# An encoder layer on one Trainium2 core: where the branches' forms are made, and when their weights and the first gate's products come

## The chip, the cores and the metric

The kernel runs on one NeuronCore of a Trainium2 chip. The metric is device time in microseconds (us) of one execution, the median of several. The engines are TensorE (PE: matmuls and transposes, results in PSUM), VectorE (DVE), ScalarE (ACT), GpSimd (POOL; here element-wise work on SBUF and a few DMA issues) and SyncE (SP, which issues the weight fetches). Each engine takes its own instructions strictly in the order of the program; they wait for each other by semaphores.

## The reference, cut to what matters

One layer on 512 tokens of width 1024: a mixer, a cross-attention into 256 memory tokens and a SwiGLU, each behind an RMS norm and added to the residual. The change touches the mixer:

```
p = h @ w_in                    # h: normed x, 512 x 1024
q, k, v, z, cb, cc, cx, gates = split(p)
ya = stick_breaking_attention(q, k, v)
u, v = split(gelu(z)); v = layer_norm(v, ln_g, ln_b)
yb = u * (w_spatial @ v + b_spatial)     # the spatial unit: 4 groups of 128 channels, 128 positions
yc = cb * conv3(cc * cx)
merged = sum over n of sigmoid(gates[n]) * (y[n] @ w_branch[n])
out = merged @ w_out
```

## The kernel before

**Arithmetic.** Matmuls are in fp32r. Each fp32 operand is cut in two: `wh` is the cast (ACT), `wl` the remainder, operand minus cast (DVE); `split` and `cut` write both. A product is three matmuls: high x high, high x low, low x high. `hT` (pair `hTh`, `hTl`) is the normed input, transposed, 8 row blocks x 512 tokens.

**Buffers.** Raw weights come by SP into `wr`, a ring of three 1 MB tiles in the pool `wp`. Their halves go into `wh` and `wl`, rings of six each. PSUM has eight banks: four turn about in `bank()`, four are the accumulators `acc`.

**The order** on each engine is made by a scheduler from the program's order and its own estimate of times; what is wrapped in `pin(...)` keeps its place.

**The spatial unit.** `nat_gemm` multiplies four token tiles of 128 rows by a 1024 x 512 weight (two raw tiles, four pieces of two row blocks). First come the columns of v (`sgu_v`): Gelu, statistics, the scale on DVE, gain and bias on POOL with `lng` and `lnb`, and the cut into `vlh`, `vll`. Then `w_spatial` (`wsr`) is transposed (`pws`) and cut into `wsh`, `wsl`. Then come the columns of u (`sgu_u`): a Gelu of each tile into `un`. Then `pg`, the spatial product of each of four groups, is multiplied into `un` on DVE, and `sgu_turn` transposes `un` (`pgt`) into `yb` (`ybh`, `ybl`).

**The branches.** Twelve items (three branches x four pieces of 256 gate columns) compute a gate and a branch product each. The first item's gate is a plain product (`gts`, two column tiles). The other eleven run in `seven_run` by a scheme of seven half-size products in place of eight. It needs sums and differences of the quarters of the weights (made per item) and of `hT` (made once, the "forms" t1 to t4). `right_forms(k)` makes the forms of row blocks k and k + 4: POOL adds `hTh` and `hTl` back into fp32, four DVE subtractions make the forms, and a cast and a remainder write them to `hTth`, `hTtl`. Its work tile `f` has eight parts and is taken from the ring `wr`. It is called for k = 0 to 3 behind the Gelus of the u tiles.

An item's branch product `pbr` (`extra_mul`, 24 matmuls) uses its piece of `w_branch`, fetched into `wb` and cut by `extra_cut`. Behind the last item the output product `pb` begins, in four accumulators.

Of the kernel before, what the change touches and what calls it, by code (L numbers as in the profile page):

```python
# [17 lines left out]
def encoder_kernel(  # L18
# [9 lines left out]
    nc = tc.nc  # L28
# [108 lines left out]
    def gemm(dst, lh, ll, rh, rl, ks, first=True, last=True):  # L137

        n, tot = 0, 3 * len(ks)
        for a, b in ((lh, rh), (lh, rl), (ll, rh)):  # L140
            for i, j in ks:
                nc.tensor.matmul(dst, a(i), b(j), start=first and n == 0, stop=last and n == tot - 1)  # L142
                n += 1
# [3 lines left out]
        gemm(dst, lambda i: w[0][:, i, :], lambda i: w[1][:, i, :],  # L147
             lambda i: act[0][:, i, cs], lambda i: act[1][:, i, cs], [(i, i) for i in range(k)])

    def nat_gemm(w, col0, act, ntt, evac, raws=(None, None), ready=None):  # L150

        pieces = []
        for c in range(2):
            pieces += w_rows(w, 4 * c, 4, col0, raws[c])
        if ready is not None:
            ready()
        for t in range(ntt):
            dst = bank(nm("pn"))
            gemm(dst,
                 lambda i: act[0][:, i, t * P:(t + 1) * P], lambda i: act[1][:, i, t * P:(t + 1) * P],  # L160
                 lambda i: pieces[i // 2][0][:, i % 2, :], lambda i: pieces[i // 2][1][:, i % 2, :],
                 [(i, i) for i in range(KD)])
            evac(t, dst)

    ALLT = slice(0, T)
# [143 lines left out]
    def seven_run(items, fill=lambda i: None, at=None, then=None):  # L309

        z = len(items)
        for k in range(z + 1):
            n = items[k] if k < z else None
            p = items[k - 1] if k else None
            q = items[k + 1] if k + 1 < z else None
            if k == at:
                got = then()
            if k + 2 < z:
                items[k + 2].load()
            if n:  # L320
                n.a, n.c = n.tile_a(), n.tile_a()
                n.mul(n.a, "l11", "r11", True, False)
            if q:
                q.sums()
            if n:
                y = n.hi(("s3", "l22"), n.right)
                n.m1 = n.keep("m1")
                n.lo(y)
                n.mul(n.c, "s1", "t1", True, False)
            if k == z:  # L330
                fill(0)
            if p:
                p.gate22()
                p.mul(p.c, "s4", "r22", False, True)
            if k == z:
                fill(1)
            if q:
                x = q.hi(("l11", "l12"), q.left)
                q.lo(x)
                c = q.hi(("s1",), q.s1)  # L340
            if p:
                p.c12(p.c[:, 0:256], p.u2)
            if n:
                n.mul(n.a, "s2", "t2", False, False)
                n.u2 = n.keep("u2")
            if q:
                q.sums2()
                q.lo(c)
            if k > 1:
                items[k - 2].extra_out()  # L350
            if p:
                p.done0()
                p.mul(p.a, "l22", "t4", False, True)
            if q and not q.late:
                b = q.hi(("s2", "s4"), q.left)
            if p:
                p.c21(p.a[:, 0:256])
                p.extra_cut()
            if n:
                n.extra_load()  # L360
                bk = bank(nm("pfb"))
                n.mul(bk, "l12", "r21", True, True)
            if q and q.late:
                n.c11(bk[:, 0:256], n.m1)
                b = q.hi(("s2", "s4"), q.left)
            if q and k:
                q.lo(b)
            if n:
# [12 lines left out]
        return got if then else None  # L381
# [273 lines left out]
    vl = tuple(up.tile([P, NT, W], F32R, name=f"vl{s}") for s in "hl")  # L655

    def sgu_v(t, dst):
        zt = up.tile([P, W], F32, name=nm("zt"), tag="zt", bufs=2)
# [5 lines left out]
        rs = rstd_of(mv[:, 1:2], 1e-5, 1.0)  # L664
        nc.vector.tensor_scalar(out=zt, in0=zt, scalar1=mv[:, 0:1], scalar2=rs, op0=ALU.subtract, op1=ALU.mult)
        nc.gpsimd.tensor_tensor(out=zt, in0=zt, in1=lng, op=ALU.mult)
        nc.gpsimd.tensor_tensor(out=zt, in0=zt, in1=lnb, op=ALU.add)
        split(zt, vl[0][:, t, :], vl[1][:, t, :])

    def right_forms(k):  # L670
        f = wp.tile([P, 8, T // 2], F32, name=nm("wr"), tag="wr", bufs=3)
        r11, r12, r21, r22, t1, t2, t3, t4 = (f[:, i, :] for i in range(8))
        for i, kk in ((0, k), (2, k + 4)):
            nc.gpsimd.tensor_tensor(out=f[:, i:i + 2, :], in0=hT[0][:, kk, :].rearrange("p (a b) -> p a b", a=2),
                                    in1=hT[1][:, kk, :].rearrange("p (a b) -> p a b", a=2), op=ALU.add)
        for o, a, b in ((t1, r12, r11), (t3, r22, r12), (t2, r22, t1), (t4, r21, t2)):
            nc.vector.tensor_tensor(out=o, in0=a, in1=b, op=ALU.subtract)
# [9 lines left out]
    split(dst.rearrange("p (g t) -> p g t", g=CT), ws[0], ws[1])  # L687
    un = up.tile([P, NT, W], F32, name="un")

    def sgu_u(t, dst):  # L690
# [14 lines left out]
    def sgu_turn():  # L705
        for g in range(CT):
# [2 lines left out]
                nc.tensor.transpose(dst[:, n * P:(n + 1) * P], un[:, n, g * P:(g + 1) * P], ident)  # L709
            split(dst, yb[0][:, g, :], yb[1][:, g, :])  # L710

    sgu_turn()
    close(up)

# [4 lines left out]
    acc = lambda: psm.tile([P, 512], F32, name=nm("pf"), tag="acc", bufs=4)  # L719
    BR = ((2, yc), (1, yb), (0, ya))  # L720
    mt_ = []

    class Branch(Seven):
# [64 lines left out]
        def extra_out(self):  # L788
            if self.n == 2:
# [3 lines left out]
                for d in ds:  # L793
# [14 lines left out]
    for j in range(2):  # L808
        pgt = bank(nm("pgt"))
        col_gemm(pgt, gts[j], hT, ALLT)  # L810
        nc.scalar.activation(out=it.g[:, j, :], in_=pgt, func=AF.Sigmoid)
    items = [Branch(n, c) for n in range(3) for c in range(4)][1:]
    seven_open(items)
    it.extra_mul()
# [435 lines left out]
```

## Time and profile before

| | |
|---|---|
| time, median of 3 runs | 978.65 us (977.56, 978.65, 983.42) |
| the profiled execution | 980.02 us; its span, first to last instruction, 978.3 us |
| mean granted clock of TensorE | 0.992 |
| busy: PE, DVE, ACT, POOL | 956.6, 647.1, 462.2, 233.4 us |
| the stage in question | u product from 201.99, first `pbr` at 246.37, last item's `pbr` from 417.17 |

Times in the rows are us from the start of the span. A row of the timeline gives the start, the duration, engine, line, operation, written tile <- read tiles (buffer numbers left out), shape and count of instructions merged into it; in square brackets stands the idle time of the engine before it and what ended that. A row of matmuls is longer than the distance to the next row, since matmuls overlap. PEld is the loading of weights into PE; "SPq" is the issue of a DMA. The busy shares and the waits are sums over the whole span; a stage is read from the timeline.

### The profile page before, as it was taken

The page shows a single profiled execution, that of the slowest core. Times are in us where ns is not written, and L with a number is a line of the kernel's source. Part 1 is how long each engine was busy: PE and PEld are TensorE (multiplying, and loading weights), DVE is VectorE, ACT ScalarE, POOL GpSimd, SP SyncE. Part 2 cuts the span into 40 slices and gives each one's busy share as a digit, 9 for nine tenths or more (in the row PEclk, how much of TensorE's full clock was granted, in tenths as well). Part 3 has the DMA queues.
Part 4 walks back from the last instruction along what each step waited for, and adds up shares of the span by engine and source line. Part 5 has one row for each costly group of instructions (what it writes and reads, how often), then busy time and mean ns, then how long its engine had stood idle before and what let it go on. Part 6 is the DMA issues. An engine that isn't in the chain of part 4 may idle for free. (4 is left out here: it accounts for less than half of the span.)

```text
span 978.3 us, 14467 instructions
## 1 busy us (share of the span) xinstructions
PE 956.6 (98%) x5942; PEld 859.1 (88%) x5942; DVE 647.1 (66%) x815; ACT 462.2 (47%) x724; POOL 233.4 (24%) x207
## 2 busy tenths in 40 slices
PE   7999999989999999999999999999999999999997
PEld 7988888868999999878988888899999999988885
DVE  6677887883766666566845545599888888772313
ACT  6474665433534345355735434555555455651301
POOL 1221123451311535220000000044444545100000
PEclk8999999989999999999999999999999999999999
DMA  8421221151223323272544121114243433533102
GB/s 294 138 87 45 84 87 44 33 172 43 87 88 125 111 88 108 87 264 80 173 149 153 47 84 44 49 39 130 87 129 90 127 92 124 172 130 90 61 1 86
DMA packets 80514, 100.83 MB, mean 103 GB/s; under 512 B 2000, under 2 KB 63488, under 8 KB 80448
## 3 DMA queue, kind: packets, MB, share of 16 engines
q1 hardware_dynamic: 79200, 95.45, 30.0%
q0 software_dynamic: 1248, 4.46, 1.3%
q8 instruction: 46, 0.75, 0.3%
q14 instruction: 20, 0.16, 0.0%
HBM read 97.80 MB, written 2.10 MB: 102 GB/s over the span
## 5 line engine op out<-in xcount | busy, mean ns | idle before, releaser
L105 DVE TENSOR_TENSOR wl<-wr,wh 128x1024 fp32r<-128x1024 f32 x100 | 122.4, 1234 | 109.3 <-ACT wh L104 83.5
L270 DVE TENSOR_TENSOR wl<-wr,wh 128x1024 fp32r<-128x1024 f32 x93 | 135.8, 1471 | 38.2 <-ACT wh L265 38.2
L104 ACT CAST wh<-wr 128x1024 fp32r<-128x1024 f32 x100 | 103.6, 1050 | 113.0 <-PE pb L142 61.4
L265 ACT CAST wh<-wr 128x1024 fp32r<-128x1024 f32 x93 | 97.7, 1052 | 26.4 <-DVE wr L255 26.4
L172 POOL TENSOR_TENSOR rs<-ve,mhalf 128x1 f32<-128x1 f32 x22 | 15.0, 682 | 325.7 <-DVE ve L170 325.7
L248 POOL TENSOR_TENSOR s<-wr 128x512 f32<-128x512 f32 x31 | 40.8, 1315 | 131.4 <-DVE w L270 118.2
L284 ACT COPY u<-pf 128x256 f32<-128x256 f32 x62 | 23.1, 373 | 92.0 <-DVE g L1078 31.5
L249 POOL TENSOR_TENSOR wr<-wr 128x512 f32<-128x512 f32 x31 | 63.7, 2056 | 2.4
L142 PE MATMUL pb<-wh,aTh 128*128 128x512 f32 x152 | 47.0, 389 | 0.0
L786 POOL TENSOR_TENSOR merged<-merged,sg 128x512 f32<-128x512 f32 x16 | 27.6, 1726 | 81.0 <-DVE sg L785 81.0
L142 PE MATMUL pb<-wl,aTh 128*128 128x512 f32 x152 | 46.8, 389 | 0.0
L142 PE MATMUL pb<-wh,aTl 128*128 128x512 f32 x152 | 46.3, 389 | 0.0
L578 POOL TENSOR_SCALAR_AFFINE_SELECT ab<-ab 128x128 f32<-128x128 f32 x32 | 23.8, 777 | 80.1 <-ACT ab L575 80.1
L867 DVE TENSOR_TENSOR xr<-pb,xr 128x512 f32<-128x512 f32 x24 | 16.1, 687 | 33.4 <-PE pb L142 33.1
L278 PE MATMUL pf<-h3th,wh 128*128 128x256 f32 x240 | 37.1, 277 | 0.4 <-ACT m L284 0.4
L278 PE MATMUL pf<-h3tl,wh 128*128 128x256 f32 x240 | 37.0, 276 | 0.0
L278 PE MATMUL pf<-h3th,wl 128*128 128x256 f32 x240 | 37.0, 276 | 0.0
L181 ACT ACTIVATE jk<-xr 128x512 f32<-128x512 f32 x24 | 15.1, 630 | 45.4 <-DVE xr L867 45.2
L142 PEld LDWEIGHTS pb<-wh,aTh 128*128 128x128 f32 x152 | 28.5, 188 | 5.9
L142 PEld LDWEIGHTS pb<-wl,aTh 128*128 128x128 f32 x152 | 28.5, 188 | 5.9
L142 PEld LDWEIGHTS pb<-wh,aTl 128*128 128x128 f32 x152 | 28.5, 188 | 5.9
L284 ACT COPY m<-pf 128x256 f32<-128x256 f32 x31 | 11.6, 373 | 46.9 <-PE pf L278 44.6
(322 smaller groups left out, 2512.6 us busy)
## 6 DMA issues: line engine op xcount, KB each, us to landing
wr<-in_w_in_dram SPq DMA_DIRECT2D x26, 1024.0 KB, 5.2
wr<-in_w_gate_ffn_dram SPq DMA_DIRECT2D x11, 1024.0 KB, 5.3
wr<-in_w_up_ffn_dram SPq DMA_DIRECT2D x11, 1024.0 KB, 5.3
wr<-in_w_down_ffn_dram SPq DMA_DIRECT2D x10, 1024.0 KB, 5.1
wb<-in_w_branch_dram SPq DMA_DIRECT2D x12, 512.0 KB, 3.3
wr<-in_w_out_dram SPq DMA_DIRECT2D x4, 1024.0 KB, 5.4
wr<-in_w_k_xa_dram SPq DMA_DIRECT2D x4, 1024.0 KB, 6.7
wr<-in_w_v_xa_dram SPq DMA_DIRECT2D x4, 1024.0 KB, 5.0
```

The costliest lines, as they stand in the source:

```text
L104: nc.scalar.copy(out=hi, in_=src)
L105: nc.vector.tensor_tensor(out=lo, in0=src, in1=hi, op=ALU.subtract)
L142: nc.tensor.matmul(dst, a(i), b(j), start=first and n == 0, stop=last and n == tot - 1)
L248: pin(nc.gpsimd.tensor_tensor(out=self.s1, in0=r[:, 0:4, P:256], in1=r[:, 4:8, P:256], op=ALU.add))
L249: pin(nc.gpsimd.tensor_tensor(out=r[:, 0:4, P:256], in0=r[:, 0:4, 0:P], in1=r[:, 0:4, P:256], op=ALU.subtract))
L265: pin(nc.scalar.copy(out=t[0], in_=src))
L270: pin(nc.vector.tensor_tensor(out=l, in0=src, in1=h, op=ALU.subtract))
L278: pin(nc.tensor.matmul(dst[:, 0:256], w[:, k, :], v[:, k, :], start=first and n == 0, stop=last and n == 11, skip_group_check=True))
L284: pin(nc.scalar.copy(out=m, in_=self.a[:, 0:256]))
L578: nc.gpsimd.affine_select(out=dg, in_=dg, compare_op=ALU.is_gt, fill=0.0, base=0, channel_multiplier=1, pattern=[[-1, P]])
L786: pin(nc.gpsimd.tensor_tensor(out=merged[:, d, :], in0=merged[:, d, :], in1=sg, op=ALU.add))
L867: nc.vector.tensor_tensor(out=xr[t][:, cs], in0=self.dsts[t], in1=xr[t][:, cs], op=ALU.add)
```

## The change

- The forms' work tile has four parts and is written in place. It is no longer taken from the ring `wr` but lies in the memory of the spatial unit's `wsr` and `ln` (`lng` and `lnb` in one tile), by turns.
- POOL's additions for the forms stand behind the last v tile's norm; the casts stand behind the Gelu of the third u tile (k = 0) and of the fourth (the others).
- The first u tile's product is written in two parts, by halves of the weight.
- The first gate's weights are fetched and cut ahead of `sgu_turn`, and its first column tile's product is written there, into an accumulator.
- In `seven_run`, the last item's `extra_cut` stands ahead of its sigmoids.
- The forms lie in the order t1, t3, t4, t2; their values stay the same.

```diff
-    def nat_gemm(w, col0, act, ntt, evac, raws=(None, None), ready=None):
+    def nat_gemm(w, col0, act, ntt, evac, raws=(None, None), ready=None, parts=1):
...
         for t in range(ntt):
             dst = bank(nm("pn"))
-            gemm(dst,
...
-                 [(i, i) for i in range(KD)])
+            m = parts if t == 0 else 1
+            for q in range(m):
+                gemm(dst,
...
+                     [(i, i) for i in range(q * KD // m, (q + 1) * KD // m)], first=q == 0, last=q == m - 1)
             evac(t, dst)
...
             if k == z:
+                p.extra_cut()
                 fill(0)
...
                 p.c21(p.a[:, 0:256])
-                p.extra_cut()
+                if k < z:
+                    p.extra_cut()
...
-    lng = up.tile([P, W], F32, name="lng")
-    lnb = up.tile([P, W], F32, name="lnb")
-    wsr = up.tile([P, CT, P], F32, name="wsr")
+    ln = up.tile([P, 2, W], F32, name="ln", tag="ln")
+    lng, lnb = ln[:, 0, :], ln[:, 1, :]
+    wsr = up.tile([P, 2 * CT, P], F32, name="wsr", tag="wsr")[:, 0:CT, :]
...
-        nc.gpsimd.tensor_tensor(out=zt, in0=zt, in1=lnb, op=ALU.add)
+        norm_end[t] = nc.gpsimd.tensor_tensor(out=zt, in0=zt, in1=lnb, op=ALU.add)
...
     def right_forms(k):
-        f = wp.tile([P, 8, T // 2], F32, name=nm("wr"), tag="wr", bufs=3)
-        r11, r12, r21, r22, t1, t2, t3, t4 = (f[:, i, :] for i in range(8))
+        f = up.tile([P, 4, T // 2], F32, name=nm("f"), tag=("wsr", "ln")[k % 2])
+        r11, r12, r21, r22 = (f[:, i, :] for i in range(4))
         for i, kk in ((0, k), (2, k + 4)):
-            nc.gpsimd.tensor_tensor(...)
+            with tc.issue_after(norm_end[NT - 1].ins):
+                nc.gpsimd.tensor_tensor(...)
-        for o, a, b in ((t1, r12, r11), (t3, r22, r12), (t2, r22, t1), (t4, r21, t2)):
+        for o, a, b in ((r11, r12, r11), (r12, r22, r12), (r22, r22, r11), (r21, r21, r22)):
             nc.vector.tensor_tensor(out=o, in0=a, in1=b, op=ALU.subtract)
-        split(f[:, 4:8, :], hTt[0][:, :, k, :], hTt[1][:, :, k, :])
+        with tc.issue_after(un_end[(2, 3, 3, 3)[k]].ins):
+            nc.scalar.copy(out=hTt[0][:, :, k, :], in_=f)
+        nc.vector.tensor_tensor(out=hTt[1][:, :, k, :], in0=f, in1=hTt[0][:, :, k, :], op=ALU.subtract)
...
     def sgu_u(t, dst):
-        nc.scalar.activation(out=un[:, t, :], in_=dst, func=AF.Gelu)
-        for k in ((0, 1), (2,), (3,), ())[t]:
+        un_end[t] = nc.scalar.activation(out=un[:, t, :], in_=dst, func=AF.Gelu)
+        for k in ((), (), (0,), (1, 2, 3))[t]:
             right_forms(k)
-    nat_gemm(w_in, 3 * W, hT, NT, sgu_u, raws=u_raw)
+    nat_gemm(w_in, 3 * W, hT, NT, sgu_u, raws=u_raw, parts=2)
...
+    gts = w_cols(w_in, 8 * W + 2 * D)
+    pgts = []
+    def first_gate(j):
+        pgts.append(acc())
+        col_gemm(pgts[j], gts[j], hT, ALLT)
+    first_gate(0)
     sgu_turn()
...
-    for i in range(4):
-        rights[f"t{i + 1}"] = tuple(v[:, i] for v in hTt)
+    for i, n in enumerate((1, 3, 4, 2)):
+        rights[f"t{n}"] = tuple(v[:, i] for v in hTt)
...
-    gts = w_cols(w_in, 8 * W + BR[0][0] * D)
...
     for j in range(2):
-        pgt = bank(nm("pgt"))
-        col_gemm(pgt, gts[j], hT, ALLT)
-        nc.scalar.activation(out=it.g[:, j, :], in_=pgt, func=AF.Sigmoid)
+        if j:
+            first_gate(j)
+        nc.scalar.activation(out=it.g[:, j, :], in_=pgts[j], func=AF.Sigmoid)
```

Where the instructions stand now, at three places. In the rows, numbers behind a name tell buffers apart; each of the two programs has its own numbers and lines.

On PE, where the u product begins: before, the first token tile runs through all four weight pieces at once (`wh_1857` and `wh_1861` are the first half of the u weights, `wh_1865` and `wh_1869` the second).

```order
L686 MATMUL pws<-ident,wsr 128x128 x4
L142 MATMUL pn_1873<-wh_1857,hTh 128x512 x2
L142 MATMUL pn_1873<-wh_1861,hTh 128x512 x2
L142 MATMUL pn_1873<-wh_1865,hTh 128x512 x2
L142 MATMUL pn_1873<-wh_1869,hTh 128x512 x2
L142 MATMUL pn_1873<-wl_1858,hTh 128x512 x2
```

The same place of the changed program (first half 1856 and 1860, second 1864 and 1868; `pn_1898` is the second token tile):

```order
L696 MATMUL pws<-ident,wsr 128x128 x4
L142 MATMUL pn_1872<-wh_1856,hTh 128x512 x2
L142 MATMUL pn_1872<-wh_1860,hTh 128x512 x2
L142 MATMUL pn_1872<-wl_1857,hTh 128x512 x2
L142 MATMUL pn_1872<-wl_1861,hTh 128x512 x2
L142 MATMUL pn_1872<-wh_1856,hTl 128x512 x2
L142 MATMUL pn_1872<-wh_1860,hTl 128x512 x2
L142 MATMUL pn_1898<-wh_1856,hTh 128x512 x2
L142 MATMUL pn_1872<-wh_1864,hTh 128x512 x2
```

The second half is read fourteen matmuls into the product instead of four.

On ACT, over the same time, before (`zt` is a Gelu of the v product, `wr_1685` the second half of the u weights, `wr_2068` the first gate's weights):

```order
L659 ACTIVATE zt_1752<-pn_1727 128x512
L104 CAST hTth<-wr_1943 128x4x256
L104 CAST hTth<-wr_1978 128x4x256
L104 CAST vlh<-zt_1712 128x512
L104 CAST wh_1865<-wr_1685 128x1024
L104 CAST wh_1869<-wr_1685 128x1024
L104 CAST wh_2070<-wr_2068 128x1024
L104 CAST vlh<-zt_1752 128x512
L659 ACTIVATE zt_1792<-pn_1767 128x512
```

and now (`wr_1684` and `wr_2032` are the same weights):

```order
L665 ACTIVATE zt_1751<-pn_1726 128x512
L104 CAST vlh<-zt_1711 128x512
L665 ACTIVATE zt_1791<-pn_1766 128x512
L104 CAST vlh<-zt_1751 128x512
L104 CAST wh_1864<-wr_1684 128x1024
L104 CAST wh_1868<-wr_1684 128x1024
L104 CAST wh_2034<-wr_2032 128x1024
L665 ACTIVATE zt_1831<-pn_1806 128x512
```

The forms' casts are gone from here, and the v tiles' casts and Gelus have moved ahead of the weights' cuts. The forms' casts stand further on, the last of them between the first and second `ybh`, with the table load, the first gate's sigmoid and the cut of `wb` behind:

```order
L703 ACTIVATE un<-pn_1959 128x512
L687 CAST hTth<-f_1985 128x4x256
L687 CAST hTth<-f_1994 128x4x256
L104 CAST ybh<-pgt_2067 128x512
L687 CAST hTth<-f_2003 128x4x256
L104 CAST ybh<-pgt_2074 128x512
L104 CAST ybh<-pgt_2081 128x512
L104 CAST ybh<-pgt_2088 128x512
L830 ACT_TABLE_LOAD
L830 ACTIVATE sg_2102<-pf_2042 128x512
L786 CAST wh_2103<-wb_2100 128x1024
```

On DVE, from the last v tile's remainder on: before, the four products with `pg` and the four `ybl` follow at once. Now the forms (`f_1950`, `f_1985`, `f_1994`, `f_2003` for k = 0 to 3) stand among them:

```order
L105 TENSOR_TENSOR vll<-zt_1831,vlh 128x512
L685 TENSOR_TENSOR f_1950<-f_1950 128x256
L105 TENSOR_TENSOR wsl<-pws,wsh 128x512
L685 TENSOR_TENSOR f_1950<-f_1950 128x256 x3
L685 TENSOR_TENSOR f_1985<-f_1985 128x256 x4
L688 TENSOR_TENSOR hTtl<-f_1950,hTth 128x4x256
L685 TENSOR_TENSOR f_1994<-f_1994 128x256 x2
L714 SCALAR_TENSOR_TENSOR un<-pg_2012,chan,un 128x4x128
L685 TENSOR_TENSOR f_1994<-f_1994 128x256
L714 SCALAR_TENSOR_TENSOR un<-pg_2017,chan,un 128x4x128
L688 TENSOR_TENSOR hTtl<-f_1985,hTth 128x4x256
L685 TENSOR_TENSOR f_1994<-f_1994 128x256
```

Each `un`, which PE's transposes read, now has subtractions of the third and fourth group or remainders of the first ahead of it.

More of the change, by code (lines that the diff above doesn't have):

```diff
@@ L158, in nat_gemm @@
             dst = bank(nm("pn"))
-            gemm(dst,
-                 lambda i: act[0][:, i, t * P:(t + 1) * P], lambda i: act[1][:, i, t * P:(t + 1) * P],
-                 lambda i: pieces[i // 2][0][:, i % 2, :], lambda i: pieces[i // 2][1][:, i % 2, :],
-                 [(i, i) for i in range(KD)])
+            m = parts if t == 0 else 1
+            for q in range(m):
+                gemm(dst,
+                     lambda i: act[0][:, i, t * P:(t + 1) * P], lambda i: act[1][:, i, t * P:(t + 1) * P],
+                     lambda i: pieces[i // 2][0][:, i % 2, :], lambda i: pieces[i // 2][1][:, i % 2, :],
+                     [(i, i) for i in range(q * KD // m, (q + 1) * KD // m)], first=q == 0, last=q == m - 1)
             evac(t, dst)
@@ L655, in encoder_kernel @@
     vl = tuple(up.tile([P, NT, W], F32R, name=f"vl{s}") for s in "hl")
+    norm_end = {}
     def sgu_v(t, dst):
@@ L666, in sgu_v @@
         nc.gpsimd.tensor_tensor(out=zt, in0=zt, in1=lng, op=ALU.mult)
-        nc.gpsimd.tensor_tensor(out=zt, in0=zt, in1=lnb, op=ALU.add)
+        norm_end[t] = nc.gpsimd.tensor_tensor(out=zt, in0=zt, in1=lnb, op=ALU.add)
         split(zt, vl[0][:, t, :], vl[1][:, t, :])
     def right_forms(k):
-        f = wp.tile([P, 8, T // 2], F32, name=nm("wr"), tag="wr", bufs=3)
-        r11, r12, r21, r22, t1, t2, t3, t4 = (f[:, i, :] for i in range(8))
+        f = up.tile([P, 4, T // 2], F32, name=nm("f"), tag=("wsr", "ln")[k % 2])
+        r11, r12, r21, r22 = (f[:, i, :] for i in range(4))
         for i, kk in ((0, k), (2, k + 4)):
-            nc.gpsimd.tensor_tensor(out=f[:, i:i + 2, :], in0=hT[0][:, kk, :].rearrange("p (a b) -> p a b", a=2),
-                                    in1=hT[1][:, kk, :].rearrange("p (a b) -> p a b", a=2), op=ALU.add)
-        for o, a, b in ((t1, r12, r11), (t3, r22, r12), (t2, r22, t1), (t4, r21, t2)):
+            with tc.issue_after(norm_end[NT - 1].ins):
+                nc.gpsimd.tensor_tensor(out=f[:, i:i + 2, :], in0=hT[0][:, kk, :].rearrange("p (a b) -> p a b", a=2),
+                                        in1=hT[1][:, kk, :].rearrange("p (a b) -> p a b", a=2), op=ALU.add)
+        for o, a, b in ((r11, r12, r11), (r12, r22, r12), (r22, r22, r11), (r21, r21, r22)):
             nc.vector.tensor_tensor(out=o, in0=a, in1=b, op=ALU.subtract)
-        split(f[:, 4:8, :], hTt[0][:, :, k, :], hTt[1][:, :, k, :])
+        with tc.issue_after(un_end[(2, 3, 3, 3)[k]].ins):
+            nc.scalar.copy(out=hTt[0][:, :, k, :], in_=f)
+        nc.vector.tensor_tensor(out=hTt[1][:, :, k, :], in0=f, in1=hTt[0][:, :, k, :], op=ALU.subtract)
     u_raw = []
@@ L688, in encoder_kernel @@
     un = up.tile([P, NT, W], F32, name="un")
+    un_end = {}
     def sgu_u(t, dst):
-        nc.scalar.activation(out=un[:, t, :], in_=dst, func=AF.Gelu)
-        for k in ((0, 1), (2,), (3,), ())[t]:
+        un_end[t] = nc.scalar.activation(out=un[:, t, :], in_=dst, func=AF.Gelu)
+        for k in ((), (), (0,), (1, 2, 3))[t]:
             right_forms(k)
-    nat_gemm(w_in, 3 * W, hT, NT, sgu_u, raws=u_raw)
+    nat_gemm(w_in, 3 * W, hT, NT, sgu_u, raws=u_raw, parts=2)
     for g in range(CT):
@@ L710, in sgu_turn @@
             split(dst, yb[0][:, g, :], yb[1][:, g, :])
+    acc = lambda: psm.tile([P, 512], F32, name=nm("pf"), tag="acc", bufs=4)
+    gts = w_cols(w_in, 8 * W + 2 * D)
[4 more added lines that the diff above has]
+    first_gate(0)
     sgu_turn()
@@ L718, in encoder_kernel @@
     gate2 = lambda: gp.tile([P, 2, T], F32, name=nm("sg"), tag="sg", bufs=2)
-    acc = lambda: psm.tile([P, 512], F32, name=nm("pf"), tag="acc", bufs=4)
     BR = ((2, yc), (1, yb), (0, ya))
```

## The prediction, made before the changed kernel was run

> **What bounds the kernel now.** I read the busy shares first.
>
> ```profile
> PE 956.6 (98%) x5942; PEld 859.1 (88%) x5942; DVE 647.1 (66%) x815; ACT 462.2 (47%) x724; POOL 233.4 (24%) x207
> ```
>
> TensorE (PE) works 98% of the span, and the change neither adds nor removes a matmul. So only the time in which PE stands still or runs slowly can be won. The list of waits, for PE alone, says where that is.
>
> ```profile
> PE pn L142 <- ACT wh L104: 4.3, 1, 4.3
> PE pbr L778 <- ACT wh L766: 1.8, 1, 1.8
> PE pf L278 <- DVE sg L736: 0.5, 1, 0.5
> ```
>
> The columns are total wait, times, longest. The first (`pn`, the spatial unit's products) and the second (`pbr`, the branches' own products) are single stalls, both on the stretch that the change touches. The timeline of PE shows what surrounds the first.
>
> ```profile
> 199.81 1.99 PE L142 MATMUL pn<-wh,hTl 128*128 128x512 f32 x8
> 201.99 1.18 PE L142 MATMUL pn<-wh,hTh 128*128 128x512 f32 x4
> 207.46 2.17 PE L142 MATMUL pn<-wh,hTh 128*128 128x512 f32 x4 [4.29 <-ACT wh L104]
> 209.43 3.19 PE L142 MATMUL pn<-wl,hTh 128*128 128x512 f32 x8
> 212.45 2.01 PE L142 MATMUL pn<-wh,hTl 128*128 128x512 f32 x8
> 214.30 1.98 PE L142 MATMUL pn<-wh,hTh 128*128 128x512 f32 x8
> ...
> 219.74 1.98 PE L142 MATMUL pn<-wh,hTh 128*128 128x512 f32 x8
> ...
> 230.62 0.39 PE L142 MATMUL pg<-vlh,wsh 128*128 128x512 f32 x1
> ```
>
> An undisturbed token tile of 24 matmuls takes 219.74 - 214.30 = 5.44 us, 0.227 each. The u product has four such tiles, 21.76 us; begun at 201.99 it should end at 223.75, and `pg` starts at 230.62. **6.87 us** are lost there: 4.29 of waiting, and the twelve matmuls from 207.46 to 212.45 take 0.416 each, 2.27 more than they should. The windows say why.
>
> ```profile
> 205.00:210.00 5.00, 2.54 (x6) 1.82 (x7) 4.03 (x4) 5.00 (x7) 3.25 (x2) 0.51 0.68 220
> 415.20:417.20 2.00, 0.21 (x3) 0.04 (x1) 0.82 (x3) 2.00 (x5) 1.67 (x4) 1.00 0.58 115
> ```
>
> The third number from the right is PE's granted clock: 0.51 in the window of the 4.29 us stall and of the slow matmuls, 1.00 through the shorter stall near 416. A stall of this length is paid about one and a half times. (The Trainium skill, "TensorE: Matmul & The Clock Gate", Part 1: The HAM clock gate, has this as a rule: after an idle window of about 3.4 us the clock is halved until a busy window has passed. That would be an estimated 1.7 us lost at half rate, against 2.27 in the rows, and a gain 0.6 smaller; the trace agrees in kind.)
>
> Why ScalarE (ACT) was late:
>
> ```profile
> 204.45 0.41 DVE L677 TENSOR_TENSOR wr<-wr 128x256 f32<-128x256 f32 x1
> 204.90 1.04 ACT L104 CAST hTth<-wr 128x1024 fp32r<-128x1024 f32 x1 [4.08 <-DVE wr L677]
> 205.85 0.61 ACT L104 CAST vlh<-zt 128x512 fp32r<-128x512 f32 x1
> 206.37 2.94 ACT L104 CAST wh<-wr 128x1024 fp32r<-128x1024 f32 x3
> 152.22 0.37 SPq L113 DMA_DIRECT2D wr<-in_w_in_dram  x1
> 202.37 0.37 SPq L113 DMA_DIRECT2D wr<-in_w_in_dram  x1
> ```
>
> The u weights' second half had been fetched since 152.22 (the last weight fetch before 202.37, and the order has it ahead of the gate's). It was not cut because ACT takes its instructions in turn and stood before the last form's cast (`hTth`), which waited for VectorE's (DVE) subtraction. The first of the three cuts ends at 207.4, where PE resumes.
>
> **The change part by part.**
>
> *Forms leave the queue ahead of the u weights.* No `hTth` now stands before the second half's cuts. What bounds them next is their destination: six `wh` buffers, and these cuts reuse those of the v product's weights, whose last matmuls are the eight in the row at 199.81. The first two of these end at about 200.3; so I take three cuts from there to 203.2 (2.94 us for x3, above), and their `wl` 1.2 us behind each (a remainder of this shape takes 1.23, in a row below), the second at 203.8. With the first token tile in two parts, PE meets the second half fourteen matmuls after 201.99, at 205.2, and its last `wl` at about 208. Cover 4 us: the stall and the slow matmuls go, **-6.87 us**. If the cover were gone, the old stall would come back in part, but then only above 4 us of delay. Fetching sooner (the gate's weights no longer wait for a form's buffer until 202.37) adds nothing itself: in the old trace PE did not wait for them.
>
> *What is late next: the fourth u tile.* Its bank is free once `wsl` is cut, and this now stands on DVE behind the last norm and the first form subtraction.
>
> ```profile
> 212.92 0.60 ACT L659 ACTIVATE zt<-pn 128x512 f32<-128x512 f32 x1 [1.68 <-DVE vll L105]
> 223.71 0.69 DVE L105 TENSOR_TENSOR wsl<-pws,wsh 128x512 fp32r<-128x512 f32 x1
> ```
>
> From the last norm's Gelu to `wsl` before: 212.92 to 224.40, 11.5 us, with two tiles' norms in it. The Gelu now follows the three cuts, at 203.2. Adding one POOL addition and a subtraction (prices below, 1.9 at most and 0.4) gives 217.0; PE comes to that tile at 201.99 + 3 x 5.44 = 218.3. Free, by 1.3 us; 4 if only one tile's norm is in the chain.
>
> *The forms, now behind the norm.* The same four groups, each of two POOL additions, four subtractions, an ACT cast and a DVE remainder, in place instead of in an eight-part tile. Their prices:
>
> ```profile
> 169.04 3.78 POOL L674 TENSOR_TENSOR wr<-hTh,hTl 128x512 f32<-128x512 f32 x2
> 195.89 2.70 POOL L674 TENSOR_TENSOR wr<-hTh,hTl 128x512 f32<-128x512 f32 x2
> 173.30 0.41 DVE L677 TENSOR_TENSOR wr<-wr 128x256 f32<-128x256 f32 x1
> 193.99 1.50 DVE L677 TENSOR_TENSOR wr<-wr 128x256 f32<-128x256 f32 x1 [1.17 <-POOL wr L674]
> 205.97 1.23 DVE L105 TENSOR_TENSOR hTtl<-wr,hTth 128x1024 fp32r<-128x1024 f32 x1 [1.11 <-ACT hTth L104]
> 231.58 2.73 DVE L702 SCALAR_TENSOR_TENSOR un<-pg,chan,un 128x512 f32<-128x512 f32 x4 [7.17 <-PE pg L142]
> 233.99 2.05 ACT L104 CAST ybh<-pgt 128x512 fp32r<-128x512 f32 x4 [2.58 <-PE pgt L709]
> 236.67 1.05 ACT L766 CAST wh<-wb 128x1024 fp32r<-128x1024 f32 x1 [0.63 <-DMA wb<-in_w_branch_dram]
> 237.74 1.28 ACT L811 ACT_TABLE_LOAD   x1
> 241.13 0.60 ACT L811 ACTIVATE sg<-pgt 128x512 f32<-128x512 f32 x1 [2.10 <-PE pgt L142]
> ```
>
> An addition costs 1.35 to 1.9 us, a subtraction 0.41 alone and up to 1.5 beside a POOL addition. Two buffers serve four groups, so the third waits for the first's remainder and the fourth for the second's. PE, without the stall, ends u at 223.75, and in the new order runs nine `pg` matmuls, thirteen of the gate, three `pg`, eleven of the gate (231.9), twelve transposes (233.4), five of the gate (234.5), four transposes (235.0), and nineteen of the gate (239.35); then `pbr`. Against it I walk the chain with additions at 1.6 and overlapped subtractions at 1.2 to 1.5:
> - third u tile done 218.3, its Gelu 219.1 (0.60 and 0.2 of latency); first form's cast 220.1, remainder 221.3;
> - POOL's third group 221.4 to 224.6; DVE's subtractions and two `un` of 0.69 to 226.7; second remainder 227.9;
> - POOL's fourth group to 231.2; third remainder 232.2; last `un` 232.9, ahead of PE's transposes at 234.5;
> - last subtractions 234.1, last form's cast 235.15. Behind this cast ACT has three `ybh` (236.7), the table load (238.0), the first gate's sigmoid (238.6) and the cut of `wb` (239.6).
>
> `pbr` wants that cut at 239.35: **+0.3 us**, with 0 at the cheap prices (additions 1.35: 238.75) and 1.5 when everything runs at the dear end while POOL works. The `wl` half is wanted eight matmuls later and is there. The gate's 13 matmuls ahead of the last `pg` cover the fourth u Gelu. The forms are first read at about 246, ten microseconds behind the last remainder.
>
> *The last item's cut of `wb` comes sooner.*
>
> ```profile
> 414.76 0.62 PE L278 MATMUL pf<-hTth,wl 128*128 128x256 f32 x4
> 417.17 1.19 PE L778 MATMUL pbr<-yah,wh 128*128 128x512 f32 x4 [1.79 <-ACT wh L766]
> 416.08 1.03 ACT L766 CAST wh<-wb 128x1024 fp32r<-128x1024 f32 x1
> 412.60 0.69 DVE L785 TENSOR_TENSOR sg<-pbr,sg 128x512 f32<-128x512 f32 x1 [2.03 <-PE pbr L778]
> 407.42 0.37 SPq L762 DMA_DIRECT2D wb<-in_w_branch_dram  x1
> wb<-in_w_branch_dram SPq DMA_DIRECT2D x12, 512.0 KB, 3.3
> ```
>
> PE could start `pbr` at 415.21 (four of these matmuls take 0.45) and starts at 417.17: **-1.96 us**. The fetch lands at 407.4 + 3.3 = 410.7, so the cut ahead of the sigmoids can end at 411.7, its `wl` on DVE behind the row at 412.60, at 414.5. What is pushed back are the last item's two sigmoids, behind some seven casts of 1 us on ACT. Their readers come after `pbr`, and the two accumulators that they hold are the third and fourth of the next product, which the new order puts behind the whole of `pbr`. Cost 0.
>
> **Sum.** -6.87 + 0.3 - 1.96 = -8.5 us. The profiled execution (980.02, span 978.3) would be 971.5 with a span of 969.8; the median shown is 978.65, so **970.1 us**. Behind both places PE is bound by its own work, so the shift reaches the end whole. If the 0.3 is not paid and the 0.5 stall of the third row of waits goes too, the gain is 9.4: a ceiling.
>
> **Rivals.**
> 1. *A new wait takes a part back.* The chain above ends in ACT's queue with hardly any cover. For it: subtractions of 1.50 beside additions, and forms, `un` and `ybl` alternate on DVE. Against it: POOL's additions fill only half of that time. One to four more microseconds: 971.5 to 975.
> 2. *Slower: the chain runs at the contended price throughout.* With additions at 1.9, every subtraction at 1.5 and the remainders longer by the same 1.1, the steps above give: first remainder 222.4, POOL to 226.2, second remainder 232.9, POOL to 236.7, last `un` 239.6, last subtractions 244.1, last form's cast 245.1, cut of `wb` 249.6. PE stalls 10.2 and pays 2.3 more at half clock, 12.5 against 8.8 won: 982.3. It decides from a last form's cast at 241.4, 6.3 behind my walk. Against it: DVE is slowed only while POOL works. (The Trainium skill, "GPSIMD Engine Reference", 1. Specifications, speaks for this: GpSimd's SBUF interfaces are shared with VectorE, in contention with instructions of two SBUF inputs, as the subtractions are. The trace agrees, 1.50 against 0.41.)
> 3. *The second edit gives nothing:* a late landing of `wb` holds ACT, or a bank is late behind the pushed sigmoids. 972.1.
> 4. *The change does not do what it says for u:* the cuts find their buffers late and the first part of the tile covers only 2.7 us. Against it: the buffers' readers end by 201.6. With half the old stall, 973 to 974.
>
> **How the numbers follow.** Forecast 0.64, the first rival 0.15, the second 0.05, the third 0.1, the fourth 0.06. The range takes the ceiling (969.2) with 1 us of spread below, and the first, third and fourth rivals above: 968 to 975.5. About what a measurement of this kernel can tell from no change is 1%, here 968.9 and 988.4. The forecast lies at 0.87%, close to that: a third of its chance falls beyond 968.9 (0.23), if the cover holds everywhere and the 0.5 stall goes. Over 988.4 would need the slower rival with six more microseconds (0.03). 0.74 lies within.
>
> **What would show it.** Right: no PE wait on `wh` at the u product and a clock of 1.00 through that stretch; `pg` near 223.8; `pbr` at 239.4 to 240; no wait above 0.5 us at the last `pbr`. Wrong: a PE wait on `un` or on `wh` of `wb` near 235 to 242, the clock below 1 there, POOL additions above 1.9, or accumulators late behind the last item's sigmoids.

## The result, and the profile after

The changed kernel takes **970.4 us** (median of 6 executions, 969.35 to 974.07) beside 978.99 (6, 977.56 to 983.42): a ratio of 0.99, 95% interval 0.9874 to 0.9925. The forecast was 970.1; that it came within 0.3 us is luck, since the medians of one kernel differ by more than that from one set of executions to the next (973.67 for this one in a second set, below). The fair test of the forecast is the difference in the traces, -8.81 us where it had -8.5. By the bound of 2% that is "the same"; the interval lies below 1. The profiled execution takes 970.6 us, its span 968.9 (978.3 before).

PE's list of waits, after; the columns are total, times, longest:

```profile
PE pf L280 <- ACT m L286: 0.4, 1, 0.4
PE pbr L798 <- ACT wh L786: 0.4, 1, 0.4
```

The 4.3 us on `pn`, the 1.8 us on `pbr` and the 0.5 us on `sg` are gone, and the second line is new. (The other lines of the list are those of the start and of stages that the change does not touch.) The timeline of PE, after, at the marks between which I compare, and the last mark in the trace of before:

```profile
201.49 1.18 PE L142 MATMUL pn<-wh,hTh 128*128 128x512 f32 x4
...
223.39 0.39 PE L142 MATMUL pg<-vlh,wsh 128*128 128x512 f32 x1
...
239.49 1.19 PE L798 MATMUL pbr<-ych,wh 128*128 128x512 f32 x4 [0.40 <-ACT wh L786]
...
407.52 0.62 PE L280 MATMUL pf<-hTth,wl 128*128 128x256 f32 x4
407.98 1.08 PE L798 MATMUL pbr<-yah,wh 128*128 128x512 f32 x4
...
502.55 0.61 PE L142 MATMUL pq<-h2h,wh 128*128 128x512 f32 x2
```

```profile
511.86 0.61 PE L142 MATMUL pq<-h2h,wh 128*128 128x512 f32 x2
```

From the first u matmul to the first `pg`: 21.90 us (28.63 before). From there to the first `pbr`: 16.10 (15.75). From there to the last item's `pbr`: 168.49 (170.80). From there to the cross-attention's first `pq`: 94.57 (94.69). Together -8.81 us. 0.50 more lies ahead of the first mark (201.49 against 201.99), where one kernel's executions differ by more than that (200.31 in the changed kernel's second trace), and 0.11 behind the last, up to the end of PE's last matmul. The granted clock (third number from the right) stays at 1.00 where it was 0.51:

```profile
205.00:210.00 5.00, 5.00 (x23) 4.13 (x22) 3.57 (x7) 1.05 (x2) 1.14 (x2) 1.00 0.92 298
```

On ACT, the cuts of the u weights' second half now come ahead of the time at which PE wants them. No form's cast stands before them; what they wait for is PE, which reads the buffers that they reuse. Of the three casts in the row, two are the second half's:

```profile
199.97 2.95 ACT L104 CAST wh<-wr 128x1024 fp32r<-128x1024 f32 x3 [2.81 <-PE pn L142]
```

The chain that the prediction walked, from the timelines of POOL, DVE and ACT:

```profile
212.02 5.96 POOL L682 TENSOR_TENSOR f<-hTh,hTl 128x512 f32<-128x512 f32 x4
221.72 2.57 POOL L682 TENSOR_TENSOR f<-hTh,hTl 128x512 f32<-128x512 f32 x2 [3.74 <-DVE hTtl L688]
227.97 2.70 POOL L682 TENSOR_TENSOR f<-hTh,hTl 128x512 f32<-128x512 f32 x2 [3.68 <-DVE hTtl L688]
215.38 0.69 DVE L105 TENSOR_TENSOR wsl<-pws,wsh 128x512 fp32r<-128x512 f32 x1
215.98 4.52 DVE L685 TENSOR_TENSOR f<-f 128x256 f32<-128x256 f32 x7
220.42 1.22 DVE L688 TENSOR_TENSOR hTtl<-f,hTth 128x1024 fp32r<-128x1024 f32 x1
229.43 1.52 DVE L685 TENSOR_TENSOR f<-f 128x256 f32<-128x256 f32 x1 [0.55 <-POOL f L682]
232.01 0.74 DVE L714 SCALAR_TENSOR_TENSOR un<-pg,chan,un 128x512 f32<-128x512 f32 x1
218.81 1.05 ACT L687 CAST hTth<-f 128x1024 fp32r<-128x1024 f32 x1
234.09 1.05 ACT L687 CAST hTth<-f 128x1024 fp32r<-128x1024 f32 x1 [1.22 <-DVE f L685]
235.17 2.03 DVE L688 TENSOR_TENSOR hTtl<-f,hTth 128x1024 fp32r<-128x1024 f32 x1 [0.57 <-ACT hTth L687]
238.40 1.04 ACT L786 CAST wh<-wb 128x1024 fp32r<-128x1024 f32 x1
239.82 1.05 ACT L267 CAST wh<-wr 128x1024 fp32r<-128x1024 f32 x1
```

First remainder done at 221.64 (221.3 in the walk), last `un` 232.75 (232.9), last form's cast 235.14 (235.15), cut of `wb` 239.44 (239.6). In square brackets POOL waits twice for a remainder: two buffers serve four forms, so POOL, DVE and ACT take turns and none of them is busy throughout.

### The profile page after: what moved, and what is told of

The parts are those of the page before. It is cut to its first block, busy times and chain, and to the rows that moved or that the text cites. A ratio compares the mean times of both kernels' runs of the same rounds, so it can differ in the third digit from the quotient of the medians.

```text
span 968.9 us, 14478 instructions
## 1 busy us (share of the span) xinstructions
PE 953.5 (98%) x5942; PEld 857.1 (88%) x5942; DVE 645.2 (67%) x815; ACT 462.5 (48%) x724; POOL 231.3 (24%) x207
```

## The experiments

Ten kernels, and the changed one a second time; the kernel before ran beside each. In part of the traces the last stage's matmuls ran slower at a granted clock of 1.00, which made these up to 5 us longer (the rows are in the last section), and the medians scatter by as much. So each kernel is judged by stretches of its own trace that end ahead of that stage: from the first u matmul to the first `pbr`, and from there to the first `pq` of the cross-attention.

| kernel | u to `pg` | `pg` to `pbr` | `pbr` to `pq` | sum | time, ratio to before (95%) |
|---|---|---|---|---|---|
| before | 28.63 | 15.75 | 265.49 | 309.87 | 1 |
| after | 21.90 | 16.10 | 263.06 | 301.06 | 970.4, 0.99 (0.9874-0.9925) |
| after again | 21.90 | 16.10 | 263.07 | 301.07 | 973.67, 0.9909 (0.9876-0.9942) |
| cut alone | 28.49 | 15.77 | 263.42 | 307.68 | 981.23, 0.9994 (0.997-1.0017) |
| cut undone | 21.90 | 16.15 | 265.14 | 303.19 | 976.15, 0.9926 (0.9897-0.9955) |
| one part | 21.89 | 16.12 | 263.08 | 301.09 | 972.21, 0.9899 (0.9865-0.9932) |
| gate held | 21.89 | 17.65 | 263.44 | 302.98 | 975.93, 0.9938 (0.9912-0.9964) |
| forms alone | 21.89 | 17.82 | 267.08 | 306.79 | 978.98, 0.9961 (0.9937-0.9986) |
| forms in the ring | 30.39 | 15.13 | 262.77 | 308.29 | 979.18, 0.9966 (0.9944-0.9987) |
| additions twice | 21.89 | 27.46 | 264.78 | 314.13 | 986.65, 1.0039 (1.0018-1.0059) |
| late additions twice | 21.89 | 21.70 | 265.43 | 309.02 | 979.93, 0.9977 (0.9956-0.9999) |
| additions three times | 21.89 | 37.82 | 264.65 | 324.36 | 998.27, 1.0166 (1.0136-1.0196) |
| `wb` first | 21.89 | 15.54 | 263.66 | 301.09 | 974.01, 0.9925 (0.9901-0.9949) |

> The changed kernel as it is, beside the two others on the same chip, to compare stretches with: from the first u matmul to the first pbr 38.0 us, from there to the last pbr 173.9, and 970 to 974, depending on the pace of the last products (351 matmuls in 40 us, or 342).

The changed kernel's stretches repeat to 0.01 us, its time to 3 us. The ratios are to the kernel before beside it, whose median was 978.99 us in the first executions and 980.15 to 983.35 beside the later runs; the expectations count from the first, so most of the totals that they name are 1 to 4 us too low for that alone. In every row the difference of the sum from before, as a share of the whole, lies inside the interval of the ratio. The theory in all that follows is the prediction's: the u stall came from the forms' place in ACT's queue, the last stall from the cut's place behind two sigmoids, and the forms' new place has no slack to spare. The rivals are named in each expectation.

**The early cut of the last item, alone and undone.**

```diff
             if k == z:
+                p.extra_cut()
                 fill(0)
...
-                p.extra_cut()
+                if k < z:
+                    p.extra_cut()
```

Alone on the kernel before:

> The kernel before with the last item's cut of wb ahead of its sigmoids, nothing else. Theory (the cut's place in ACT's queue made the 1.8 us wait at the last pbr): that wait is gone, 979.0 - 1.96 = 977.0 us, and the 4.3 us wait at the u product stays. Rival (the pushed sigmoids or the landing of wb take it back): 978.5 to 979 and a new wait of PE in the first 10 us behind the last pbr.

Taken out of the changed kernel:

> The changed kernel with that cut back behind the sigmoids. Theory: the wait of 1.8 us at the last pbr returns and nothing else, 970.4 + 2.0 = 972.4 us. Rival (the gain at the end of the branches came from the earlier stage, whose weights are fetched sooner): 970.4 to 971.

PE's waits, with the cut alone and with the cut undone:

```profile
PE pn L142 <- ACT wh L104: 4.5, 2, 4.3
```

```profile
PE pbr L796 <- ACT wh L784: 2.2, 2, 1.8
```

Alone it ends the wait at the last `pbr` and leaves the one at u: `pbr` to `pq` falls by 2.07 us, the sum by 2.19. Undone, the 1.8 us are back, 2.13 in the sum (2.2 in the row includes the 0.4 at the first `pbr`). The two agree on what the cut is worth. The median of the cut alone shows no gain at all: 2 us are less than its ten executions, 975.92 to 983.57, scatter.

**The product in one part.**

```diff
-    nat_gemm(w_in, 3 * W, hT, NT, sgu_u, raws=u_raw, parts=2)
+    nat_gemm(w_in, 3 * W, hT, NT, sgu_u, raws=u_raw)
```

> The changed kernel with the first u tile in one part. Theory (the forms' place alone removed the stall): the second half of the weights is wanted eight matmuls into the product, at 203.3 in the changed kernel's trace, and its first cut ends at 201.0, its second at 202.0: no wait, 970.4 us within 0.5, and 21.8 to 22.0 us from the first u matmul to pg. Rival (the first part is the cover that hides the cuts): a wait on wh of 1 to 3 us there, 971.5 to 973.5.

21.89 us, sum 301.09: the two parts are worth nothing here, and the kernel without them is as fast. The second half of the weights is cut by the time that PE comes to it in either order.

**The first gate held back behind the transposes.**

```diff
-    first_gate(0)
     sgu_turn()
...
-        if j:
+        with tc.issue_after(turned[0].ins):
             first_gate(j)
```

`turned[0]` is the last transpose.

> The changed kernel with the first gate's products held behind the last transpose of un, as they stood before; accumulators, weights and forms as changed. Theory (these products cover the forms' chain on DVE): PE ends pg at 226.1 in the changed kernel's time and finds the last two un at about 229 and 229.7, so it waits 3 us among the transposes, ends them at 230.2 and the gate at 241.1 instead of 239.1; the 0.4 at pbr goes: 972.1 us, or 974.4 if the clock drops. Rival (the cover is not needed): 970.0 to 970.8.

PE's waits:

```profile
PE pgt L723 <- DVE un L714: 1.5, 1, 1.5
PE pf L280 <- DVE sg L757: 0.5, 1, 0.5
```

PE has nothing to put between the last `pg` and the transposes that need the last `un`. The wait is half of the 3 us that I expected. The early gate is worth 1.92 us in the sum; the wait at the first `pbr` is gone, and the 0.5 us on the gate's tile is back as before.

**The forms in their old place, the rest of the change kept.** The forms' additions and casts also lose the orders that the change gave them.

```diff
-        f = up.tile([P, 4, T // 2], F32, name=nm("f"), tag=("wsr", "ln")[k % 2])
+        f = wp.tile([P, 8, T // 2], F32, name=nm("wr"), tag="wr", bufs=3)
...
-        for k in ((), (), (0,), (1, 2, 3))[t]:
+        for k in ((0, 1), (2,), (3,), ())[t]:
```

> The changed kernel, but the four forms are again made in the ring tile of eight parts, at the old places (two behind the first u eviction, one behind each of the next two), and their POOL additions wait for nothing new. First product in two parts, early gate and early cut stay. Theory (the forms' place was the cause: the rounding of the second half of the u weights stands in ACT's queue behind a form's rounding that waits for DVE): TensorE waits again in the first u tile, but only at its second part, because twelve matmuls (2.7 us) stand ahead of it: about 2.7 us in place of 4.3, so the stretch from the first u matmul to the first pg is 24.5 to 26.9 us (21.90 in the changed kernel, 28.63 before; the upper figure if the clock halves), and the whole 973 to 975.5. Rival (the early fetch or the tiles' memory made the gain, the order of the queue is no matter): 21.9 us, 970.4.

PE and ACT there:

```profile
205.66 2.17 PE L142 MATMUL pn<-wh,hTh 128*128 128x512 f32 x4 [2.48 <-ACT wh L104]
208.27 1.22 PE L142 MATMUL pn<-wl,hTh 128*128 128x512 f32 x2 [0.45 <-DVE wl L105]
209.29 3.25 PE L142 MATMUL pf<-hTh,wh 128*128 128x512 f32 x8
...
212.85 0.62 PE L142 MATMUL pn<-wl,hTh 128*128 128x512 f32 x2
203.09 1.04 ACT L104 CAST hTth<-wr 128x1024 fp32r<-128x1024 f32 x1 [4.09 <-DVE wr L683]
204.56 2.94 ACT L104 CAST wh<-wr 128x1024 fp32r<-128x1024 f32 x3
```

The order is that of before: ACT waits 4.09 us for a form's subtraction, and only then rounds the u weights. The first part shortens PE's wait to 2.5 us, as expected, and the clock falls with it: eight matmuls in 3.25 us. The stretch is longer than foretold because the scheduler puts ten matmuls of the gate into it (209.29 to 212.85, 3.56 us, most of it at half clock); without them it is 26.8. The first `pbr` then waits 1.7 us for its `wh` as well.

My rival for this run (the early fetch or the tiles' memory made the gain) is not tested by it: with the forms' tile the kernel takes back the ring, and the fetch of the first gate's weights is late again. The fetches that follow those of the u weights, the gate's first, in the changed kernel and here:

```profile
168.45 12.04 SPq L113 DMA_DIRECT2D wr<-in_w_in_dram  x2
```

```profile
200.56 0.37 SPq L113 DMA_DIRECT2D wr<-in_w_in_dram  x1
```

What speaks against the rival is the row of ACT: the u weights' second half had been fetched since 150.40 here (152.22 before), and what ACT stood before was a form's cast that waited for DVE, not a weight.

**The forms' edit alone on the kernel before.**

> The kernel before with the forms' edit alone: in place in the spatial unit's tiles, POOL additions behind the last norm, roundings behind the named Gelus. No product in parts, no early gate, no early cut. Theory (the forms carry the 6.87 us by themselves, the early gate covers the end of their chain): first u matmul to first pg 21.8 to 22.0 us with the clock at 1.00; a wait of about 1.5 us for the last un among the transposes, as where the gate was held; the first pbr waits 0 to 1 us for its rounding; the last item's wait of 1.8 us and the 0.5 us on the gate's tile stay: 973.5 to 975.5. Rival (it takes all the parts): 977 or more, with a wait of over 3 us at the first pbr.

21.89 us, at a clock of 1.00: the forms' edit (their place, their tiles, and the earlier fetch that comes with these) carries the whole gain at u by itself. The wait among the transposes is the one that the held gate showed, and the last item's 1.8 us stays; here that wait cost more than in the kernel before. Its rows of PE and its windows:

```profile
229.60 1.31 PE L716 MATMUL pgt<-ident,un 128*128 128x128 f32 x8 [1.47 <-DVE un L709]
...
412.66 1.29 PE L785 MATMUL pbr<-yah,wh 128*128 128x512 f32 x4 [1.79 <-ACT wh L773]
413.75 1.91 PE L785 MATMUL pbr<-yal,wh 128*128 128x512 f32 x4
```

```profile
415.00:420.00 5.00, 5.00 (x19) 4.07 (x18) 4.28 (x6) 2.35 (x3) 0.09 (x1) 0.80 0.92 344
```

Behind a wait of the same 1.79 us that left the clock at 1.00 before, it fell to half for a while, and `pbr` to `pq` is 1.59 us longer than before.

**The forms' additions made more often.** With `n` copies of the same addition:

```diff
             with tc.issue_after(norm_end[NT - 1].ins):
-                nc.gpsimd.tensor_tensor(...)
+                for _ in range(n):
+                    nc.gpsimd.tensor_tensor(...)
```

Twice, and three times:

> The changed kernel with each of the forms' POOL additions made twice (the same result twice): 10.4 us more work on POOL, on the chain that ends in the last form's rounding. Theory (the chain was within half a microsecond of its need): the last form's rounding moves from 234.1 to about 237, the rounding of wb from 238.4 to about 241, so TensorE waits about 1.8 us at the first pbr in place of 0.4, and the stretch from the first pg to the first pbr grows from 16.1 to 17.5 to 18 us: 971.8 to 972.4. Rival (there is more cover than that, a few microseconds of POOL cost nothing): 16.1 us, 970.4.

> The changed kernel with each of the forms' POOL additions made three times (the same result each time): some 21 us more on POOL. It looks for the point from which the prediction's slower rival would have come true: a last form's rounding behind 241.4 and a wait at the first pbr so long that the clock falls. Theory: the last form's rounding at about 247 to 249, wb rounded behind it at about 250, TensorE waits 9 to 11 us at the first pbr and then runs about 2.3 us longer at half clock: 980 to 983, the whole gain gone. Rival (the wait alone, no clock loss): 978 to 980. Rival (wb's rounding gets ahead of the form's in ACT's queue): 970 to 973.

PE, ACT and POOL with the additions twice:

```profile
235.81 0.66 PE L722 MATMUL pgt<-ident,un 128*128 128x128 f32 x4 [2.57 <-DVE un L715]
250.97 2.08 PE L799 MATMUL pbr<-ych,wh 128*128 128x512 f32 x4 [9.03 <-ACT wh L787]
246.54 1.04 ACT L688 CAST hTth<-f 128x1024 fp32r<-128x1024 f32 x1 [5.47 <-DVE f L686]
212.14 10.66 POOL L683 TENSOR_TENSOR f<-hTh,hTl 128x512 f32<-128x512 f32 x8
227.01 12.14 POOL L683 TENSOR_TENSOR f<-hTh,hTl 128x512 f32<-128x512 f32 x8 [4.21 <-DVE hTtl L689]
```

Both expectations were far too low, and both theories wrong in the same place: I thought that a few microseconds of POOL's work would hide in the pauses that its rows show. They hide nothing. Counted from the first u matmul, the last form's cast begins 12.3 us later (44.92 us where it was 32.60) for 11.6 us more of POOL's time (10.66 + 12.14, where the three rows of after sum to 11.23); PE waits 2.6 us among the transposes and 9.0 at the first `pbr`. With three times, POOL's two rows sum to 31.59 us, 20.4 more, and that cast begins 22.7 us later; PE waits 21.8 us at the first `pbr` (9 to 11 expected), and the kernel is slower than before by 1.7%:

```profile
PE pbr L799 <- ACT wh L787: 21.8, 1, 21.8
```

**The point between.** Additions twice for the third and fourth form alone, `range(1 + k // 2)`:

> The changed kernel with the POOL additions of the third and fourth form alone made twice (the same result twice), 5.3 us more on the chain. With all four doubled the last form's rounding came 12.4 us later and the whole was slower than before. This one looks for the point between: the prediction let the change lose from a last form's rounding at 241.4. Theory (the chain has no slack, each microsecond on it is one of waiting at the first pbr or at the transposes, and about 2 more once the clock falls): last form's rounding at 239.5 to 241, waits of 5.5 to 7 us in sum, from the first u matmul to the first pbr 43.5 to 45.5 us (38.00 in the changed kernel, 44.38 before), and the whole 976 to 978.5, close to before, the last microseconds of the gain being those at the last item. Rival (part of the second and fourth form's time was hidden, the loss lay in the first two): under 41 us, 972 to 973.5.

POOL, ACT and PE there, and the window behind the wait:

```profile
220.81 5.11 POOL L683 TENSOR_TENSOR f<-hTh,hTl 128x512 f32<-128x512 f32 x4 [3.74 <-DVE hTtl L689]
227.41 5.66 POOL L683 TENSOR_TENSOR f<-hTh,hTl 128x512 f32<-128x512 f32 x4 [1.50 <-DVE hTtl L689]
239.76 1.04 ACT L688 CAST hTth<-f 128x1024 fp32r<-128x1024 f32 x1 [4.76 <-DVE f L686]
244.18 2.07 PE L799 MATMUL pbr<-ych,wh 128*128 128x512 f32 x4 [5.41 <-ACT wh L787]
```

```profile
245.00:250.00 5.00, 5.00 (x13) 3.84 (x13) 4.35 (x6) 2.51 (x4) 1.27 (x1) 0.51 0.35 107
```

As the theory had it: waits of 5.4 us there and 0.4 among the transposes, 43.59 us to the first `pbr`, then half clock, which costs 2.37 us in `pbr` to `pq`. 5.5 us more of POOL's time (10.77 in the two rows, 5.27 after) move the last form's cast by 6.6 us and undo 7.96 of the 8.81 us.

**`wb` ahead of the first gate's sigmoids.**

```diff
-        nc.scalar.activation(out=it.g[:, j, :], in_=pgts[j], func=AF.Sigmoid)
+        with tc.issue_after(it.cut_.ins):
+            nc.scalar.activation(out=it.g[:, j, :], in_=pgts[j], func=AF.Sigmoid)
```

`it.cut_` is the cast of `wb`.

> The changed kernel with one more order on ACT: the first gate's two sigmoids are issued behind the rounding of the first item's wb, with which the table load (1.28 us) goes behind it too. Theory (the 0.4 us wait at the first pbr is ACT's queue alone: last form's rounding, three ybh, table load, sigmoid, wb): wb is rounded by about 237.7, the wait is gone, and the stretch from the first u matmul to the first pbr falls from 38.00 to 37.6 us; the gate's tile is read at 246.6 and the sigmoids end by 241, so nothing else waits: 970.0, not to be told from the changed kernel by the time. Rival (wb lands late or the sigmoids' readers wait): 38.0 us or more, and a new wait behind the first pbr.

ACT, and PE 15 us later:

```profile
235.64 1.07 ACT L786 CAST wh<-wb 128x1024 fp32r<-128x1024 f32 x1
239.00 1.05 ACT L267 CAST wh<-wr 128x1024 fp32r<-128x1024 f32 x1
254.36 0.74 PE L280 MATMUL pf<-hTh,wh 128*128 128x256 f32 x4 [0.79 <-DVE sg L756]
```

Theory and rival were each half right. The first `pbr` comes 0.56 us sooner and its wait is gone, as the theory had it; a new wait comes behind it, as the rival had it, and 0.59 us go again at the next item's gate tile: sums 301.09 and 301.07. ACT still has the same row of work ahead of the next item's operands: its cast of `wr` starts 38.37 us behind the first u matmul here (239.00 - 200.63) and 38.33 in the changed kernel (239.82 - 201.49). What PE does not wait for at `pbr`, it waits for there. So this version is no better, and no run beat the changed kernel.

## Why the prediction was right, point by point

- **The u product, -6.87:** measured -6.73. It lies in the forms' edit (alone it gives the gain whole, and with the forms back in the ring the gain is gone) and, by ACT's rows, in their place in its queue; 2.27 of it was the clock, which stays at 1.00. (The prediction's 4.29 and 2.27 make 6.56 of its 6.87. Most of the rest lies ahead of the stall: the row of four matmuls at 201.99 takes 1.18 us, where four that follow one another take 0.91.) The two parts, which I gave a role in the cover, have none. That the fetch by itself adds nothing was not tested alone. It rests on the rows: in the kernel before, PE resumed when ACT had cut weights that had been fetched since 152.22.
- **The fourth u tile:** `wsl` at 216.07 where I had 217.0, wanted at 217.9. Free, as said.
- **The new wait, +0.3 (0 to 1.5):** measured +0.35, with a walk that is within half a microsecond at every step in the rows' times, and within 0.9 counted from the first u matmul, which came 0.5 us sooner. That it came out so well is partly luck, since two errors cancel. The additions of the third and fourth form took 1.28 and 1.35 us where I took 1.6, and by my own bound (no wait at 1.35) the wait should have been 0. DVE used up what POOL saved: the first remainder starts at 220.42, 0.56 us behind the end of its cast, because the second form's subtractions stand ahead of it, which the walk left out; and from POOL's last addition to the last form's cast it is 3.4 us (230.67 to 234.09) where the walk has 2.9. So the lower bound was too low by about 1 us. The subtractions beside additions took up to 1.53, as taken.
- **Two waits that were one:** my sum left the 0.5 us stall on the gate's tile where it was, beside the 0.3, and my ceiling took both away. The runs show one in place of the other. The stall goes because the 0.35 is paid (0.36 of it, from the first `pbr` to the last item's), and comes back when the wait goes (`wb` first, 0.79 us; gate held, 0.5). Both are PE waiting for one row of ACT's work. So the new wait cost nothing in the end, and my ceiling of 9.4 could not be reached in that way. That 0.36 is missing in my sum of -8.5; the other terms, each off by less than 0.2, bring the difference to 0.3. That the two waits are one fits all thirteen traces: each has either a wait at the first `pbr` or the stall on the gate's tile, and none has both.
- **The last item's cut, -1.96:** -1.95 between the last `pf` and `pbr`, and nothing lost behind it (94.57 against 94.69): the pushed sigmoids cost 0, as said.
- **The slower rival:** its mechanism is real: POOL's time on this chain comes out whole at its end. I let it decide from a last form's cast that ends 39.4 us behind the first u matmul (241.4 - 201.99). With the late additions twice that cast ends at 40.2 and the sum is 309.02, just under the 309.87 of before; with all of them twice it ends at 46.0 and the sum is 314.13. A line between the two crosses before's sum at 41.2, an estimate, so that the point lies 1.8 us further off than I had it. About 1 us of this is that in the longer chains the three `ybh` stand ahead of that cast and a second sigmoid behind it, so that less lies between it and the cut of `wb` (3.3 us with the late additions twice, 4.3 in the changed kernel). The price of the clock, 2.3, was 2.37. What I held against this rival, that DVE is slowed only while POOL works, is so; but the chain ended 7.5 us ahead of that point (at 33.65 us, 235.14 - 201.49) and it took 5.5 to 11.6 us more of POOL's time, half or all of the additions again, to bring it near or past that point. So it was the price of the additions that kept the rival out, and not slack on the way.
- **Contention:** subtractions beside POOL's additions take 1.5 us in place of 0.41, remainders 2.03 in place of 1.22, each longer by 0.8 to 1.1 us, which is most of one addition (1.28 to 1.49). The Trainium skill, "SBUF — State Buffer", SBUF: two separate sides, describes the shared ports as an exclusive lock, held for a whole instruction; whichever of the two engines comes second is blocked. The rows agree: the subtraction begun at 229.43 ends at 230.95, 0.28 us behind the end of POOL's last addition (227.97 + 2.70 = 230.67), so what is added is the rest of one addition, not a share.

## What to carry to other kernels

A cast that waits for another engine does harm through what is queued behind it, so look for the first instruction behind it that the bottleneck needs, and move the waiting one behind that. Where two or three engines hand a buffer to each other in turn, their pauses are not slack: price a microsecond added to one of them as a whole one at the end (tried here on POOL alone). And before removing a short new wait, look whether the same engine's row of work will be waited for again a little later; then it is worth nothing.

## What the runs showed of the hardware

**The clock falls behind short waits, sometimes.** Waits of 1.79 us left it at 1.00 in the kernel before and with the cut undone, and brought it to half with the forms alone (0.80 in the window above); 1.68 us at the first `pbr` left it at 1.00 with the forms in the ring, where 2.48 us at u brought it to 0.52. The window behind the 1.79 us with the cut undone:

```profile
410.00:415.00 5.00, 5.00 (x24) 4.12 (x23) 5.00 (x5) 4.21 (x5) 0.00 (x0) 1.00 0.99 350
```

Beyond the wait itself, longer waits were not dearer: behind 5.4 us, `pbr` to `pq` was 2.37 us longer than in the changed kernel, behind 9.0 us 1.72, behind 21.8 us 1.59. The Trainium skill, "TensorE: Matmul & The Clock Gate", Part 1: The HAM clock gate, has the clock halve after an idle window of about 3.4 us, in windows that run freely and do not start with the wait. That the outcome differs for equal waits fits windows that run freely; that 1.79 us were enough does not fit the full idle window, and the measurement decides.

**The last stage has two paces.** A window of 160 us in the SwiGLU, in the changed kernel and in the one with one part:

```profile
680.00:840.00 160.00, 159.85 (x1395) 158.75 (x1394) 133.56 (x159) 85.68 (x145) 70.53 (x46) 1.00 0.37 117
```

```profile
680.00:840.00 160.00, 160.00 (x1365) 159.88 (x1365) 131.97 (x156) 82.78 (x139) 70.50 (x46) 1.00 0.35 110
```

and one group of matmuls in it, in the same two (behind the bar: busy us, mean ns, idle):

```profile
L280 PE MATMUL pf<-h3th,wl 128*128 128x256 f32 x204 | 31.4, 276 | 0.0
```

```profile
L280 PE MATMUL pf<-h3th,wl 128*128 128x256 f32 x196 | 31.0, 280 | 0.0
```

1395 matmuls against 1365, 276 ns against 280, with PE busy and the granted clock at 1.00 in both. From the first `pq` to the end of PE's last matmul that is 459.3 us against 463.3 (up to 464.6 in others). Before, after (twice) and the forms in the ring ran at the faster pace, and some traces lie between. Each kernel but the changed one was traced once, so the traces do not show whether the pace changes from one execution to the next; the times of one kernel, 969.35 to 975.3 for the changed one, spread as widely. What sets it stays open. It is worth up to half of what this change brought, so here a change of 2 us is read from the stretches of a trace, not from medians.
